# Four matmuls that share one weight load, in a sliding-window matmul on TensorE

## The chip, the cores and the metric

The kernel runs on one core of one Trainium2 chip. The metric is the time of one execution on the device, in microseconds (us); the profile of one execution gives a slightly shorter span, from its first to its last instruction.

## The reference

```python
def reference(x, w, offsets):          # x (4, 4096, 4096) f32, w (4096, 4096) f32
    results = []
    for b in range(4):
        o = int(offsets[b])
        results.append(x[b, o:o+64] @ w)
    return np.stack(results)           # (4, 64, 4096) f32
```

Four windows of 64 rows make 256 rows. They are multiplied by one matrix w of 64 MB. So w is read once, and each part of it is used for only 256 rows.

## The kernel before

The 256 rows are two row halves (g = 0, 1) of 128. They are transposed at the start, so that for each of the 32 k tiles (128 rows of w each) a 128x128 block of xT is the stationary operand ("the weights" in what follows) and w is the moving operand. The output columns are done in two groups (ng) of 2048. Within one group each k tile has 2 row halves times 4 column blocks of 512 columns, that is 8 matmuls into the kernel's 8 PSUM tiles (`bank0` to `bank7` in the program, "banks" below); the four column blocks of a row half use the same weights. Most loads of w (26 of 36) bring two k tiles (1024 KB as f16, from f32) on GpSimd's queue, into 12 rotating buffers.

```python
    def load(ng, ki, n):
        t = wh_pool.tile([P, n * NG], fp16, name="wh", tag="wh")      # 12 buffers
        nc.gpsimd.dma_start(out=..., in_=w[ki * P : (ki + n) * P, ng * NG : (ng + 1) * NG]...)
        for i in range(n):
            wh[(ng, ki + i)] = t[:, i * NG : (i + 1) * NG]
    ...                                       # all loads of w are issued here; x is transposed
    def mm(g, j, ki, rhs, start, stop):
        nc.tensor.matmul(
            out=ps[4 * g + j][:],
            lhsT=xT[g][:, ki * P : (ki + 1) * P],
            rhs=rhs,
            start=start,
            stop=stop,
        )
    ...
    for ng in range(n_ng):
        last = ng == n_ng - 1
        for ki in range(n_k):
            for g in range(G):
                for j in range(n_sub):
                    mm(g, j, ki, wh[(ng, ki)][:, j * NT : (j + 1) * NT], ki == 0, ki == n_k - 1)
        for j in range(n_sub):
            for g in range(G):                # ScalarE evicts half 0, VectorE half 1
                ...
        ...                                   # store both halves
```

## Time and profile before

| | before |
|---|---|
| time | 183.54 us (3 runs, 183.46 to 183.56) |
| span of the profile | 182.0 us |
| TensorE matmuls busy | 122.8 us, 67% |
| weight loads busy (their own track, overlapping the matmuls) | 56.5 us, 31% |
| idle of TensorE ended by a load of w | 32.7 us |

In the profile PE stands for the matmuls of TensorE, PEld for its weight loads, DVE for VectorE, ACT for ScalarE, POOL for GpSimd and SP for SyncE; a q after such a name is that engine's sequencer. "<-" names what ended a wait, and "issue" is time in which an engine waited for nothing that the profile shows. The granted clock, named below, is the share of full speed that TensorE was given.

First the page's two parts on the DMA queues (kind: packets, MB, share of the time of 16 engines) and on the chain of waits that ended last (share of the span, by engine, then by line):

```profile
q0 software_dynamic: 9120, 36.70, 97.0%
...
DMA 88%; issue 3%; POOL 1%; DVE 1%; POOLq 1%; PE 1%; DVEq 0%
DMA wh<-in_w_dram 88%; DVE stage L133 1%; POOL wh L58 1%; PE bank L108 1%; POOLq L72 1%; POOL xrow L79 0%; DVEq L164 0%; POOL identity masks.py:197 0%; POOLq L79 0%; POOLq L58 0%; POOLq masks.py:199 0%; POOLq L153 0%
```

The queue that loads w keeps the DMA engines busy 97% of the time, and the work that ended last is, for 88% of the span, loads of w. Next the groups of instructions of the main loop (busy us, mean ns of one, then the idle time just before them and what ended it):

```profile
L108 PE MATMUL bank<-wh,xT 128*128 128x512 f16 x496 | 112.0, 379 | 32.7 <-DMA wh<-in_w_dram 32.7
L108 PEld LDWEIGHTS <-xT 128*128 128x128 f16 x512 | 49.9, 98 | 98.5 <-issue 42.0
```

There is one weight load (98 ns) for each matmul: 512, of which 496 belong to this matmul group and 16 to the tiles of w that came in another way. The timeline of TensorE shows the rhythm (start, length in us, then the idle time before in brackets):

```profile
41.43 3.61 PE L108 MATMUL bank<-wh,xT 128*128 128x512 f16 x16 [1.28 <-DMA wh<-in_w_dram]
46.40 3.61 PE L108 MATMUL bank<-wh,xT 128*128 128x512 f16 x16 [1.36 <-DMA wh<-in_w_dram]
```

Every 4.9 us two k tiles of w land, TensorE does their sixteen matmuls in 3.61 us, and waits for the next. One matmul is recorded as 0.38 us long, but sixteen take 3.61 us and not 16 x 0.38 = 6.1 us, so their records overlap, and the distance between starts is (3.61 - 0.38) / 15 = 215 ns. Last, the timeline after the last load of w has landed:

```profile
171.26 1.89 PE L108 MATMUL bank<-wh,xT 128*128 128x512 f16 x8 [0.54 <-DMA wh<-in_w_dram]
171.27 1.39 PEld L108 LDWEIGHTS <-xT 128*128 128x128 f16 x7 [0.82 <-issue]
171.68 2.05 ACT L131 COPY stage<-bank 128x512 f32<-128x512 f32 x4 [73.82 <-PE bank L108]
172.54 2.48 DVE L133 COPY stage<-bank 128x512 f32<-128x512 f32 x4 [73.39 <-PE bank L108]
...
175.05 0.38 SPq L135 DMA_DIRECT2D out_dram<-stage  x1
```

Eight matmuls but only seven loads fall in this stretch: the first matmul's weights had been loaded already (a load is recorded at 170.35 us).

### The profile page before, as it was taken

To read this page: it belongs to the slowest core of one execution; us is meant where nothing else is said; L and a number is where in the kernel's file an instruction comes from. 1 tells how busy PE (TensorE), PEld (TensorE's weight loads), DVE (VectorE), ACT (ScalarE), POOL (GpSimd) and SP (SyncE) were. 2 spreads that over 40 slices of the span, in tenths; PEclk is the share of its full clock that TensorE was granted. 3 is DMA by queue.
4 is the path that set the end of the run, shared out by engine and by line. 5 is a ranking of instruction groups with operands and counts; after the bars stand their busy time and mean duration, and the time that the engine had idled before them with its cause. 6 is when DMAs were issued, how large, how long until landed. Compare 5 with 4: busy or idle time off the path is not lost.

```text
span 182.0 us, 1329 instructions
## 1 busy us (share of the span) xinstructions
PE 122.8 (67%) x576; PEld 56.5 (31%) x576; DVE 10.5 (6%) x16; ACT 13.8 (8%) x19; POOL 27.7 (15%) x48
## 2 busy tenths in 40 slices
PE   0004699777777777777988777777777587799700
PEld 0004663333333322333433333333233232343300
DVE  0002540000000000000005000000000000000040
ACT  2081430000000000000004000000000000000210
POOL 4713310111111111110221111111111010100000
PEclk9999999999999999999999999999999999999995
DMA  5999999999999999999999999999999999999995
GB/s 180 348 217 216 206 214 215 216 214 215 212 213 212 216 215 216 214 215 210 212 214 217 215 215 214 212 214 213 215 216 214 215 215 211 214 212 216 367 398 216
DMA packets 9559, 40.97 MB, mean 225 GB/s; under 512 B 722, under 2 KB 722, under 8 KB 8658
## 3 DMA queue, kind: packets, MB, share of 16 engines
q0 software_dynamic: 9120, 36.70, 97.0%
q10 hardware_dynamic: 288, 3.15, 4.6%
q1 hardware_dynamic: 146, 1.05, 1.4%
q8 instruction: 4, 0.07, 0.1%
q14 instruction: 1, 0.01, 0.0%
HBM read 71.30 MB, written 4.19 MB: 415 GB/s over the span
## 4 chain that ended last, share of the span: by engine, by line
DMA 88%; issue 3%; POOL 1%; DVE 1%; POOLq 1%; PE 1%; DVEq 0%
DMA wh<-in_w_dram 88%; DVE stage L133 1%; POOL wh L58 1%; PE bank L108 1%; POOLq L72 1%; POOL xrow L79 0%; DVEq L164 0%; POOL identity masks.py:197 0%; POOLq L79 0%; POOLq L58 0%; POOLq masks.py:199 0%; POOLq L153 0%
## 5 line engine op out<-in xcount | busy, mean ns | idle before, releaser
L108 PE MATMUL bank<-wh,xT 128*128 128x512 f16 x496 | 112.0, 379 | 32.7 <-DMA wh<-in_w_dram 32.7
L108 PEld LDWEIGHTS <-xT 128*128 128x128 f16 x512 | 49.9, 98 | 98.5 <-issue 42.0
L58 POOL DMA_DIRECT2D wh<-in_w_dram x36 | 23.8, 662 | 116.8 <-DMA wh<-in_w_dram 105.8
L94 PE MATMUL bank<-identity,xrow 128*128 128x128 f16 x64 | 7.1, 311 | 17.5 <-DMA xrow<-in_x_dram 17.5
L131 ACT COPY stage<-bank 128x512 f32<-128x512 f32 x8 | 4.1, 599 | 144.4 <-PE bank L108 144.4
L133 DVE COPY stage<-bank 128x512 f32<-128x512 f32 x8 | 5.0, 682 | 145.1 <-PE bank L108 145.1
L94 PEld LDWEIGHTS <-xrow 128*128 128x128 f16 x64 | 6.7, 147 | 17.7 <-issue 17.7
L103 DVE CAST xT<-bank 128x512 f16<-128x512 f32 x8 | 5.5, 691 | 19.4 <-PE bank L94 19.4
L105 ACT CAST xT<-bank 128x512 f16<-128x512 f32 x8 | 4.7, 586 | 7.0 <-PE bank L94 7.0
L108 PE MATMUL bank<-w0half,xT 128*128 128x512 f16 x16 | 4.2, 380 | 0.2 <-DVE stage L133 0.2
L88 ACT CAST w0half<-w0row 128x2048 f16<-128x2048 f32 x1 | 1.9, 1897 | 7.2 <-DMA w0row<-in_w_dram 7.2
L79 POOL DMA_DIRECT2D xrow<-in_x_dram x4 | 2.1, 524 | 2.1 <-issue 2.1
L135 POOL DMA_DIRECT2D out_dram<-stage x2 | 1.1, 536 | 8.2 <-DMA wh<-in_w_dram 8.2
L89 ACT CAST w0half<-w0row 128x2048 f16<-128x2048 f32 x1 | 1.9, 1892 | 0.0
L88 ACT ACT_TABLE_LOAD x1 | 1.3, 1283 | 1.3 <-PEq L153 1.3
masks.py:199 POOL TENSOR_SCALAR_AFFINE_SELECT identity<-identity 128x128 f16<-128x128 f16 x1 | 0.3, 288 | 0.1
masks.py:197 POOL MEMSET identity<- 128x128 f16 x1 | 0.2, 223 | 0.0
L153 POOL MEMSET const-float32-0.0<- 128x1 f32 x1 | 0.1, 99 | 0.4 <-issue 0.4
L153 POOL MEMSET const-uint8-127<- 128x1 uint8 x1 | 0.1, 102 | 0.0
L153 POOL MEMSET const-bfloat16-1.0<- 128x1 bf16 x1 | 0.1, 101 | 0.0
L153 POOL MEMSET const-float32-1.0<- 128x1 f32 x1 | 0.1, 99 | 0.0
## 6 DMA issues: line engine op xcount, KB each, us to landing
wh<-in_w_dram POOLq DMA_DIRECT2D x26, 1024.0 KB, 36.6
wh<-in_w_dram POOLq DMA_DIRECT2D x10, 512.0 KB, 31.3
w0row<-in_w_dram ACTq DMA_DIRECT2D x1, 2048.0 KB, 8.9
xrow<-in_x_dram POOLq DMA_DIRECT2D x4, 512.0 KB, 12.2
out_dram<-stage POOLq DMA_DIRECT2D x2, 1024.0 KB, 22.8
out_dram<-stage ACTq DMA_DIRECT2D x1, 1024.0 KB, 4.9
out_dram<-stage SPq DMA_DIRECT2D x1, 1024.0 KB, 6.0
off_t<-in_offsets_dram SPq DMA_DIRECT2D x1, 0.0 KB
```

What stands on the lines that cost most here:

```text
L58: nc.gpsimd.dma_start(out=t[:].rearrange("p (t n) -> p t n", t=n), in_=w[ki * P : (ki + n) * P, ng * NG : (ng + 1) * NG].rearrange("(t p) ...
L72: o = nc.values_load(off_i32[0:1, 2 * b : 2 * b + 1], engines=[POOL], min_val=0, max_val=S - WIN, skip_runtime_bounds_check_because="offse ...
L79: nc.gpsimd.dma_start(out=x16[g][m * WIN : (m + 1) * WIN, :], in_=x[b][bass.ds(o, WIN), :])
L88: nc.scalar.copy(out=w0_16[:, :NG], in_=w0_32[:, :NG])
L89: nc.scalar.copy(out=w0_16[:, NG:], in_=w0_32[:, NG:])
L94: nc.tensor.matmul(out=ps[t][:, i * P : (i + 1) * P], lhsT=x16[g][:, k * P : (k + 1) * P], rhs=identity[:], start=True, stop=True,)
L103: nc.vector.tensor_copy(out=dst, in_=ps[t][:])
L105: nc.scalar.copy(out=dst, in_=ps[t][:])
L108: nc.tensor.matmul(out=ps[4 * g + j][:], lhsT=xT[g][:, ki * P : (ki + 1) * P], rhs=rhs, start=start, stop=stop,)
L131: nc.scalar.copy(out=dst, in_=ps[4 * g + j][:])
L133: nc.vector.tensor_copy(out=dst, in_=ps[4 * g + j][:])
L135: (q[g] if last else nc.gpsimd).dma_start(out=out[2 * g : 2 * g + 2, :, ng * NG : (ng + 1) * NG], in_=stage[ng][g][:],)
```

## The change

Load each 128x128 block of weights once for the four matmuls that use it. The first matmul of each four is emitted as before; the other three are emitted as instructions that are flagged as not loading weights.

```diff
     def mm(g, j, ki, rhs, start, stop):
-        nc.tensor.matmul(
-            out=ps[4 * g + j][:],
-            lhsT=xT[g][:, ki * P : (ki + 1) * P],
-            rhs=rhs,
-            start=start,
-            stop=stop,
+        out_ap = ps[4 * g + j][:]
+        lhsT = xT[g][:, ki * P : (ki + 1) * P]
+        if j == 0:
+            nc.tensor.matmul(out=out_ap, lhsT=lhsT, rhs=rhs, start=start, stop=stop)
+            return
+        nc.tensor.add_instruction(
+            mybir.InstMatmult(
+                name=nc.get_next_instruction_name(),
+                start_tensor_calc=start,
+                stop_tensor_calc=stop,
+                tile_position=(0, 0),
+                tile_size=(P, P),
+                ldweights=False,
+                ins=[
+                    nc.tensor.lower_ap(rhs, opt=False),
+                    nc.tensor.lower_ap(lhsT, opt=False, for_matmul_weights=True),
+                ],
+                outs=[nc.tensor.lower_ap(out_ap)],
+            )
         )
```

## The prediction

> **What bounds the kernel now.** Loading w does. The chain of waits that ended last (182.0 us span) is 88% loads of w; TensorE matmuls of the main loop are about 1% of it. The queue table gives the software queue 97% of the DMA engines' time, and the stages between 26 and 171 us move a flat 214 to 226 GB/s (destination bytes) at a DMA share above 1. TensorE is the follower: in the timeline each 1 MB load (two k tiles) lands every 4.9 us, TensorE runs its sixteen matmuls in 3.61 us and then idles 1.23 to 1.36 us, ended each time by the next load. In all it idles 32.7 us in 30 waits for loads.
>
> **What the change removes.** 384 of 512 weight loads in the main loop, 98 ns each in the line table: about 37.5 of 49.9 us of busy time on the weight-load track. It adds nothing: same matmuls, order, banks, buffers and DMAs.
>
> **What that is worth.** Nothing on TensorE, because the loads are already hidden. Sixteen matmuls in 3.61 us, with 0.38 us for one, is (3.61-0.38)/15 = 215 ns from start to start, although every one has its own load; the last group of eight gives (1.89-0.38)/7 = 216 ns. In that last group the first matmul starts at 171.26 us with its weights already loaded; the load recorded at 171.27 us belongs to the second. [...]a full-array load fits under each matmul.
>
> **How much is on the critical path.** After the last load lands (171.22 us): five matmuls (1.25 us), four VectorE evictions (about 2.5 us) and the last store (6.0 us to landing). Only the five matmuls could shrink, at a 215 ns pitch set by 512 columns; I expect under 0.05 us. Even if TensorE gained, it would wait longer for w. If instead the fifth matmul's load were exposed (four shared matmuls not letting the next load go ahead), a group would lose about 0.1 us, 0.2 us per k tile, 0.4 us per pair against 1.23 us of idle: still hidden, and about 0.1 us at the tail.
>
> **Prediction.** 183.5 us, 8 in 10 between 182.9 and 184.2. Faster by over 2%: 0.01; within 2%: 0.97; slower by over 2%: 0.02.
>
> **What would show the steps.** Right: weight loads of the main loop x128, busy near 12.5 us; matmul mean still about 379 ns; sixteen matmuls still 3.6 us; idle before matmuls still about 32 us, ended by loads of w; last load lands near 171.2 us; chain still 88% loads. Wrong: groups of sixteen at 3.2 us or less (loads did cost something), or above 3.8 us (sharing exposes loads), or a changed DMA rate.
>
> **What would make it wrong.** A lower granted clock[...]: it is 1.00 in every stage from 26 to 171 us, and at half of it sixteen matmuls would take an estimated 15x0.43+0.6 = 7 us (twice the measured pitch), more than the 4.9 us between loads; TensorE would then bind and the kernel be some 40% slower. [...] Or matmuls without a load waiting for the whole preceding matmul, which would need over 80 ns extra per matmul (1.3 us of idle over sixteen) before the time moved.

The forecast's sum was the time of the kernel before, 183.5 us, less nothing on TensorE and less under 0.05 us in the tail (estimate). The half clock in its last paragraph is one that the profile before shows: 0.50 from 180 to 182 us, with no matmul after 173.2 us. That the distance between starts goes with the columns was measured later: 215 ns for 512, 55.7 for 128 and 29.1 for 64 (experiments 7 to 10).

## The result, and the profile after

The changed kernel takes 183.52 us (median of 6 runs, 183.44 to 183.64), the kernel before 183.55 us beside it (6 runs). The ratio is 1.000, with a 95% interval of 0.9987 to 1.0012. Here and below a ratio is the mean time of one kernel's runs over that of the other's in the same rounds, so it is not quite the ratio of the medians quoted. Executions over 1.5% slower than the fastest of the same kernel are left out of the means.

The page after, the chain of waits that ended last:

```profile
DMA 88%; issue 3%; POOL 1%; DVE 1%; POOLq 1%; PE 1%; DVEq 0%
```

The time is as predicted, and so is the chain. But the groups of the main loop are not (line 111 is the first matmul of each four, line 113 the other three):

```profile
L113 PE MATMUL bank<-wh,xT 128*128 128x512 f16 x372 | 100.4, 379 | 0.0
L111 PE MATMUL bank<-wh,xT 128*128 128x512 f16 x124 | 46.9, 378 | 32.4 <-DMA wh<-in_w_dram 32.4
L113 PEld LDWEIGHTS <-xT 128*128 128x128 f16 x384 | 37.5, 98 | 82.8 <-issue 41.3
L111 PEld LDWEIGHTS <-xT 128*128 128x128 f16 x128 | 12.5, 98 | 15.6 <-issue 0.8
```

Line 113 has 384 weight loads: the very loads that the change was to remove. 384 + 128 = 512, as before. The timeline shows them between the matmuls:

```profile
41.41 0.38 PE L111 MATMUL bank<-wh,xT 128*128 128x512 f16 x1 [1.28 <-DMA wh<-in_w_dram]
41.41 0.53 PEld L113 LDWEIGHTS <-xT 128*128 128x128 f16 x3 [1.56 <-issue]
41.62 0.81 PE L113 MATMUL bank<-wh,xT 128*128 128x512 f16 x3
...
42.05 0.10 PEld L111 LDWEIGHTS <-xT 128*128 128x128 f16 x1
```

So the change removed nothing. The listings of the two built programs say why. While the kernel is being written down there is no separate load instruction in the program at all; when the tile context closes, a pass splits each of the 576 matmuls (64 for the transposes, 512 in the main loop) into a load and a matmul that doesn't load, and it does so for the 384 that carry the flag already. Both built programs then hold 576 loads and 576 matmuls. With source line numbers left out, the two listings (all five engines, operands and waits included) are the same line for line:

```
before                                    after
L108 Matmult bank_78<-wh,xT_76 128x512    L111 Matmult bank_78<-wh,xT_76 128x512
L108 Ldweights xT_76                      L113 Ldweights xT_76
L108 Matmult bank_79<-wh,xT_76 128x512    L113 Matmult bank_79<-wh,xT_76 128x512
L108 Ldweights xT_76                      L113 Ldweights xT_76
L108 Matmult bank_80<-wh,xT_76 128x512    L113 Matmult bank_80<-wh,xT_76 128x512
```

The measured "same" is therefore a comparison of a program with itself. It says nothing yet about what sharing a load is worth. The experiments make the change for real.

### The profile page after: what moved, and what is told of

It is laid out like the page before. It is cut to its first block, busy times and chain, and to the rows that moved or that the text cites. A ratio compares the mean times of both kernels' runs of the same rounds, so it can differ in the third digit from the quotient of the medians.

```text
span 182.0 us, 1329 instructions
## 1 busy us (share of the span) xinstructions
PE 123.0 (68%) x576; PEld 56.6 (31%) x576; DVE 10.5 (6%) x16; ACT 13.8 (8%) x19; POOL 27.6 (15%) x48
## 3 DMA queue, kind: packets, MB, share of 16 engines
HBM read 71.30 MB, written 4.19 MB: 415 GB/s over the span
## 4 chain that ended last, share of the span: by engine, by line
DMA 88%; issue 3%; POOL 1%; DVE 1%; POOLq 1%; PE 1%; DVEq 0%
DMA wh<-in_w_dram 88%; DVE stage L146 1%; POOL wh L58 1%; POOLq L72 1%; POOL xrow L79 0%; PE bank L113 0%; PE bank L111 0%; DVEq L177 0%; POOL identity masks.py:197 0%; POOLq L79 0%; POOLq L58 0%; POOLq masks.py:199 0%; POOLq L166 0%
## 5 line engine op out<-in xcount | busy, mean ns | idle before, releaser
L113 PE MATMUL bank<-wh,xT 128*128 128x512 f16 x372 | 100.4, 379 | 0.0
L111 PE MATMUL bank<-wh,xT 128*128 128x512 f16 x124 | 46.9, 378 | 32.4 <-DMA wh<-in_w_dram 32.4
L111 PEld LDWEIGHTS <-xT 128*128 128x128 f16 x128 | 12.5, 98 | 15.6 <-issue 0.8
L113 PE MATMUL bank<-w0half,xT 128*128 128x512 f16 x12 | 3.7, 385 | 0.2 <-DVE stage L146 0.2
L111 PE MATMUL bank<-w0half,xT 128*128 128x512 f16 x4 | 1.8, 442 | 0.0
```

The source lines that it names most:

```text
L111: nc.tensor.matmul(out=out_ap, lhsT=lhsT, rhs=rhs, start=start, stop=stop)
L113: nc.tensor.add_instruction(mybir.InstMatmult(name=nc.get_next_instruction_name(), start_tensor_calc=start, stop_tensor_calc=stop, tile_po ...
```

## The experiments

### 1. The loads really taken out

After the tile context has closed, the loads of weights that are held already are removed from the program's list; the kernel itself is the one before. None of those removed carried a wait or a signal, which the edit asserts.

```diff
     with _tile.TileContext(nc) as tc:
         tile_sliding_window_matmul_kernel(tc, *args)
+    n_cut = 0
+    for blk in nc.main_func.blocks:
+        keep, held = [], None
+        for i in blk.instructions:
+            if type(i).__name__ == "InstLdweights":
+                key = str(i.ins[0].memref) + str(i.ins[0].offset)
+                if key == held and "xT" in key:
+                    assert not (i.sync_info and (i.sync_info.on_wait or i.sync_info.on_update))
+                    n_cut += 1
+                    continue
+                held = key
+            keep.append(i)
+        blk.instructions = keep
+    assert n_cut == 384, n_cut
```

> The kernel before, with 384 of the 512 main-loop weight loads really taken out of the finished program (the changed kernel still ran all 512). Theory A (loads are hidden under the matmuls and TensorE waits for w anyway): 128 main-loop loads in the trace, about 12.5 us busy; sixteen matmuls still 3.61 us, matmul mean 379 ns; idle before matmuls about 32 us; time 183.5 us, within 0.3 us of before. Rival B (a load delays its matmul): sixteen matmuls below 3.5 us, idle time grows by the same amount, time still about 183.5 because the last load of w lands at the same time, at most 0.1 us less at the tail. Rival C (four matmuls on shared weights keep the next load from going ahead): sixteen matmuls about 3.9 us. Rival D (weight loads help to hold the clock): granted clock below 1.00 between 26 and 171 us, matmuls start 0.43 us apart, time over 250 us. Rival E: the back end puts the loads back, 512 in the trace.

Measured: correct, 183.44 us (5 runs, 183.29 to 183.58) against 183.50 us; ratio 0.9997 (0.9983 to 1.0010). The groups, and the timeline of one pair of k tiles:

```profile
L108 PE MATMUL bank<-wh,xT 128*128 128x512 f16 x496 | 111.9, 379 | 32.3 <-DMA wh<-in_w_dram 32.3
...
L108 PEld LDWEIGHTS <-xT 128*128 128x128 f16 x128 | 12.5, 98 | 135.1 <-issue 135.1
```

```profile
41.32 3.61 PE L108 MATMUL bank<-wh,xT 128*128 128x512 f16 x16 [1.15 <-DMA wh<-in_w_dram]
41.97 0.10 PEld L108 LDWEIGHTS <-xT 128*128 128x128 f16 x1 [2.08 <-issue]
42.83 0.10 PEld L108 LDWEIGHTS <-xT 128*128 128x128 f16 x1 [0.77 <-issue]
43.69 0.10 PEld L108 LDWEIGHTS <-xT 128*128 128x128 f16 x1 [0.77 <-issue]
44.56 0.10 PEld L108 LDWEIGHTS <-xT 128*128 128x128 f16 x1 [0.77 <-issue]
```

Now there are 128 loads, one for four matmuls, 0.86 us apart. The sixteen matmuls still take 3.61 us, TensorE still waits 32.3 us for w, and the granted clock is 1.00 from 26 to 171 us as before. Theory A holds and rivals B, C, D and E fall: no cost of a load shows (3.61 us with 16 loads and with 4), the next load still starts while the matmuls before it run (at 41.97 us, with the sixteen running from 41.32 to 44.93 us), and the granted clock was 1.00 with 128 loads as with 512. The weight loads' busy share of the span went from 31% to 11% (56.5 us of 182.0 us, and 19.2 of 181.9) with no change in time.

### 2 and 3. TensorE made the bottleneck, with and without the loads

In the kernel before, a small cost of a load could hide in TensorE's idle time. So each group of four matmuls is done twice, and the eviction halves the result; now TensorE has more to do than the loads of w leave time for. Experiment 3 is the same with the redundant loads cut as in experiment 1.

```diff
-            for g in range(G):
+            for g in [0, 1, 0, 1]:            # start on the first visit of a bank, stop on the second
...
-                    nc.scalar.copy(out=dst, in_=ps[4 * g + j][:])
+                    nc.scalar.mul(out=dst, in_=ps[4 * g + j][:], mul=0.5)      # likewise on VectorE
```

> Every group of four matmuls is done twice (result halved at the eviction, so still right), all 1024 matmuls with a load of their own: TensorE needs about 7.1 us per pair of k tiles against 4.9 us between loads of w, so TensorE binds. Start of the main loop 24.3 us, 1024 matmuls at 216 ns = 221 us, about 10 us of eviction and last store: 255 us (250 to 262). If the load costs its own time (98 ns) on TensorE, the matmuls would start 314 ns apart and the time be about 355 us; the trace of before says not.

> As the doubled kernel, with 768 of its 1024 loads taken out, one load for four matmuls. TensorE binds here, so what a load costs shows at once, 768 times. Theory A (hidden): same time as the doubled kernel within 0.5%, matmuls 215 to 216 ns apart. Rival B (each load costs some ns): faster by 768 times the cost; [...]20 ns each 15 us. Rival C (sharing exposes the next load): slower by 256 times up to 98 ns, up to 25 us.

Measured: 256.03 us with all loads (4 runs, 254.00 to 256.17), 254.39 us with the loads cut (4 runs, 254.06 to 255.42), both correct; ratios to the kernel before 1.3917 and 1.3859. Timeline of TensorE and group of its loads, first with all loads, then with 768 cut:

```profile
24.31 4.19 PE L108 MATMUL bank<-w0half,xT 128*128 128x512 f16 x16
28.33 107.22 PE L108 MATMUL bank<-wh,xT 128*128 128x512 f16 x496
...
L108 PEld LDWEIGHTS <-xT 128*128 128x128 f16 x1024 | 100.4, 98 | 121.6 <-issue 1.7
```

```profile
24.12 3.62 PE L108 MATMUL bank<-w0half,xT 128*128 128x512 f16 x16
27.57 107.22 PE L108 MATMUL bank<-wh,xT 128*128 128x512 f16 x496
...
L108 PEld LDWEIGHTS <-xT 128*128 128x128 f16 x256 | 25.0, 98 | 195.6 <-issue 195.6
```

496 matmuls in a row, without a gap, take 107.22 us in both. That run of matmuls has 496 loads in the one and 124 in the other. A difference as small as 0.01 us over the 372 missing loads would show, so a load costs less than 0.03 ns (0.01 / 372) in these two profiles. The 0.8 us by which the two profiled spans differ arose before this point: the first sixteen matmuls took 4.19 us in one and 3.62 us in the other, and the run of 496 starts at 28.33 and 27.57 us. The loads are not needed for such a slow start: the sixteen matmuls on w0half, whose first eight start the main loop there, have a mean of 416 ns in experiment 1, with the loads cut, and of 380 ns in the kernel before, with all of them. The executions of one kernel differ by as much (254.00 and 256.17 us with all loads), so that is not put down to the loads.

### 4. More loads than before

This is the changed kernel with an explicit load ahead of each four and the flag on all four matmuls. It is what one would write to say "one load, four matmuls" outright, but the pass adds its own load to each matmul all the same.

```diff
         if j == 0:
-            nc.tensor.matmul(out=out_ap, lhsT=lhsT, rhs=rhs, start=start, stop=stop)
-            return
+            nc.tensor.ldweights(lhsT)
```

> The changed kernel with one explicit load ahead of each group of four and the flag on all four matmuls: the program then has 640 main-loop loads, 128 more than before. Theory A: hidden where two loads fit under one matmul (2 x 98 = 196 ns below 215 ns), at most a few ns more per group; sixteen matmuls below 3.7 us, time 183.5 us. Rival B: each extra load costs about 0.1 us, sixteen matmuls 4.0 us, still hidden behind the loads of w, time 183.5 to 183.7 us.

Measured: correct, 183.44 us (4 runs) against 183.50 us, ratio 0.9997 (0.9981 to 1.0012); 640 loads in the main loop, sixteen matmuls still 3.61 us. The timeline of the weight-load track:

```profile
41.62 0.10 PEld L111 LDWEIGHTS <-xT 128*128 128x128 f16 x1
41.66 0.70 PEld L112 LDWEIGHTS <-xT 128*128 128x128 f16 x4
```

The explicit load starts at 41.62 us and the next one 40 ns later, though each is recorded as 0.10 us long. The 98 ns are thus the length of a load's record, not how long it keeps the next one away.

### 5 and 6. Is loading w really what binds?

Experiment 5 does column block 0 of each row half twice, twenty matmuls where there were sixteen. Experiment 6 leaves out every second k tile of w and uses the tile before it in its place; its result is wrong.

```diff
 # experiment 5
-                for j in range(n_sub):
+                for j in [0, 0, 1, 2, 3]:     # bank of block 0 halved at the eviction
 # experiment 6
...                                            # tile 31 uses tile 0, which is loaded in any case
             if (ng, ki) not in wh:
-                load(ng, ki, 2 if ki < n_k - 4 - (ki % 2) else 1)
+                load(ng, ki, 1)
+                wh[(ng, ki + 1)] = wh[(ng, ki)]
```

> The kernel before with column block 0 of each row half done twice (its bank halved at the eviction, still right): twenty matmuls per pair of k tiles instead of sixteen, each with a load. Theory A (TensorE has 1.2 to 1.36 us to spare in each 4.9 us): twenty matmuls take 19 x 0.216 + 0.38 = 4.5 us, idle before matmuls falls from 32 to about 6 to 10 us, time 183.5 to 184.0 us (the tail has at most two matmuls more ahead of its last eviction, 0.4 us). Rival: if TensorE were on the critical path, 126 more matmuls at 216 ns would add up to 27 us.

> Wrong on purpose: every second k tile of w is not loaded, its matmuls use the tile before it; all 512 matmuls with their loads stay. If loading w binds, the time falls until TensorE binds: 24.3 us to the main loop, 512 matmuls at 216 ns = 111 us, 10 us of tail: 146 us (140 to 155). If TensorE or anything else but the loads of w bound the kernel, it stays near 183.5 us.

Measured: 183.59 us for experiment 5 (4 runs), correct, ratio 1.0006 (0.9990 to 1.0023); 143.5 us for experiment 6 (one run, state unknown, wrong as meant). The group of matmuls in experiment 5:

```profile
L108 PE MATMUL bank<-wh,xT 128*128 128x512 f16 x620 | 137.1, 379 | 8.1 <-DMA wh<-in_w_dram 8.1
```

A quarter more work on TensorE costs no time: it went into the idle time, which fell from 32.7 to 8.1 us. Little of that time is left: the chain that ended last is now 67% DMA and 24% TensorE. And with half the loads of w the chain that ended last turns to TensorE (in experiment 6 its lines have moved by one):

```profile
PE 77%; DMA 10%; DVE 3%; issue 3%; POOLq 1%; DVEq 0%; POOL 0%
```

So loading w bounds the kernel before, and TensorE comes next.

### 7 and 8. Matmuls of 128 columns

Does a load show when its matmul is short? Each matmul of 512 columns is cut into four of 128, each with a load of its own; experiment 8 cuts the 1920 redundant ones. Theory A2 was that load and matmul partly add up. The 54 ns in A1 are a quarter of the 215 ns.

```diff
+        for c in range(0, NT, NARROW):                          # NARROW = 128
             nc.tensor.matmul(
-                out=ps[4 * g + j][:],
+                out=ps[4 * g + j][:, c : c + NARROW],
                 lhsT=xT[g][:, ki * P : (ki + 1) * P],
-                rhs=rhs,
-                start=start,
-                stop=stop,
+                rhs=rhs[:, c : c + NARROW],
+                start=start and c == 0,
+                stop=stop and c == NT - NARROW,
```

> Each 512-column matmul of the main loop cut into four of 128 columns, each with its own load of the same weights: 2048 loads and 2048 matmuls, same arithmetic. Loads no longer fit easily: a load's record is 98 ns, though two loads of the run with more loads began only about 42 ns apart. Theory A1 (a load is hidden whenever it is shorter than the matmul, 128 columns = 54 to 56 ns against about 42): sixteen old matmuls still about 3.6 us, time 183.5 us. [...]Theory A3 (they add up, 42 + 56 = 98 ns): 2048 x 98 = 201 us + 34 us = about 235 us.

> The narrow kernel with 1920 of its 2048 loads taken out, one for sixteen matmuls of 128 columns. Under A2 and A3 TensorE is freed: 64 x 56 ns = 3.6 us per pair below 4.9 us, time back at 183.5 us, and the gain over the narrow kernel is what sharing is worth where loads show. Under A1 no difference from the narrow kernel.

Measured: 184.76 us with all loads (4 runs, ratio 1.0067) and 184.66 us with the loads cut (4 runs, ratio 1.0055), both correct. One pair of k tiles in the timeline, with the loads and without:

```profile
41.42 3.73 PE L110 MATMUL bank<-wh,xT 128*128 128x128 f16 x64 [1.23 <-DMA wh<-in_w_dram]
41.43 3.61 PEld L110 LDWEIGHTS <-xT 128*128 128x128 f16 x64 [1.35 <-issue]
```

```profile
41.45 3.73 PE L110 MATMUL bank<-wh,xT 128*128 128x128 f16 x64 [1.16 <-DMA wh<-in_w_dram]
```

64 matmuls take 3.73 us in both, which with 0.22 us for one is (3.73 - 0.22) / 63 = 55.7 ns from start to start. A1 holds: even at 128 columns, with starts 55.7 ns apart, a load recorded as 98 ns costs nothing (3.73 us with 64 loads and with 4). Both narrow kernels are about 1.2 us slower than the kernel before, and in both the last load of w lands later (172.37 against 171.22 us). In each trace it is one load of w that comes about 1 us late, before 106.14 us in experiment 7 and as the last one in experiment 8. Why was not tested; the loads of weights are not the cause, since it is there without them.

### 9 and 10. Matmuls of 64 columns

The same with NARROW = 64: 4096 matmuls, with 4096 loads or with 128.

> Each 512-column matmul of the main loop cut into eight of 64 columns, each with its own load: 4096 loads and 4096 matmuls. At 128 columns a load was still free (64 matmuls in 3.73 us with and without, 55.7 ns apart). A matmul of 64 columns takes an estimated 55.7/2 = 28 ns; two loads of the run with more loads began 42 ns apart, so the load should now set the pitch: 128 x 42 = 5.4 us per pair of k tiles against 4.9 us between loads of w, TensorE binds, 4096 x 42 = 172 us + 34 us = about 206 us (195 to 225), and idle before matmuls nearly gone. If the load were hidden even here, the pair would take about 3.6 to 3.8 us and the time be 184 to 187 us[...].

> The 64-column kernel with 3968 of its 4096 loads taken out, one for 32 matmuls. If the load set the pitch, TensorE is freed: 128 x 28 = 3.6 us per pair, idle before matmuls back near 30 us, time 184 to 187 us, some 10% below the 64-column kernel with loads: the case in which the change pays. If the matmuls of 64 columns are limited by their own issue (above 38 ns each), TensorE still binds and the gain is smaller or none.

Measured: 211.49 us with all loads (4 runs, ratio 1.1537, 1.1517 to 1.1557), 185.85 us with the loads cut (4 runs, ratio 1.0120, 1.0100 to 1.0139), both correct. Here cutting the loads is worth 12%. The sizes are near what was expected, but the reason expected is wrong, so the near hit is luck. The timeline of TensorE with all loads, with the line of its weight-load track for the same stretch:

```profile
42.77 3.89 PE L110 MATMUL bank<-wh,xT 128*128 128x64 f16 x128 [2.58 <-issue]
42.77 3.80 PEld L110 LDWEIGHTS <-xT 128*128 128x128 f16 x128 [2.67 <-issue]
...
117.50 1.04 PE L110 MATMUL bank<-w0half,xT 128*128 128x64 f16 x30
120.57 1.15 PE L110 MATMUL bank<-w0half,xT 128*128 128x64 f16 x34 [2.03 <-issue]
...
180.06 21.68 PE L110 MATMUL bank<-wh,xT 128*128 128x64 f16 x738 [0.93 <-issue]
```

and with the loads cut:

```profile
41.45 3.89 PE L110 MATMUL bank<-wh,xT 128*128 128x64 f16 x128 [1.00 <-DMA wh<-in_w_dram]
```

128 matmuls take 3.89 us in both, with 0.19 us for one (3.89 - 0.19) / 127 = 29.1 ns from start to start. Loads that start (3.80 - 0.10) / 127 = 29.1 ns apart still do not slow the matmuls. What costs the time is that TensorE stands still, mostly for 2.0 to 2.6 us, after every 128 matmuls up to 180 us, for nothing that the profile shows ("issue"): 26 waits, 46.0 us in all. It is not a wait for w: one of the gaps falls between the 30th and the 34 other matmuls of a tile that had been in the buffer since the start. And the gaps end at 180 us, after which 738 matmuls run without one. 128 matmuls with 128 loads are 256 instructions, and the queue table of this run has 32 instruction packets with 0.52 MB, that is 16 KB each; the kernel before has 4 packets and 7168 instructions fewer (1024 matmuls and loads in the main loop against 8192), which is 256 instructions for each of the 28 more packets. With the loads cut there are 17. The queue lines of experiments 9 and 10:

```profile
q8 instruction: 32, 0.52, 0.9%
q8 instruction: 17, 0.28, 0.5%
```

### 11. What the gaps of the 64-column kernel are

In experiment 9 there is a 16 KB instruction packet for every 256 instructions, and a gap after every 128 matmuls with their 128 loads. The author's estimate from these counts was that the gaps are waits for the packets, which come late while the loads of w fill the DMA engines (DMA share 1.06 from 26 to 171 us). If so, the gaps should go when the loads of w go. Experiment 11 is the 64-column kernel with all its weight loads, with half the loads of w as in experiment 6 (wrong).

> The 64-column kernel with all its loads, but every second k tile of w not loaded (wrong on purpose, as in the half-bytes run), to tell what its gaps are. In its trace 128 matmuls took 3.89 us with loads as without (29 ns apart), yet TensorE then stood idle 2.0 to 2.6 us for nothing the profile shows, once per 128 loads and 128 matmuls; the queue table has 32 instruction packets of 16 KB[...]; and the gaps were gone for the last 738 matmuls, when the loads of w had ended. Theory F (the gaps are instruction fetch queued behind the loads of w): here the loads of w end near 95 us; gaps before that, none after; from then on about 29 ns per matmul, so 24.3 + 68 us with gaps (some 1470 matmuls at 5.92 us per 128) + 2600 x 0.0294 = 77 us + 10 us: about 180 us. Rival G (TensorE cannot issue more than 256 instructions in 5.92 us): gaps all the way, 211 us. Rival H (the gaps are waits for w that the profile does not show): with half the loads none anywhere, about 155 us.

Measured: 179.03 us (one run, state unknown, wrong as meant); expected about 180. The timeline of TensorE:

```profile
49.45 5.39 PE L111 MATMUL bank<-wh,xT 128*128 128x64 f16 x128 [2.03 <-issue]
55.37 3.89 PE L111 MATMUL bank<-wh,xT 128*128 128x64 f16 x128 [0.53 <-issue]
...
81.97 21.68 PE L111 MATMUL bank<-wh,xT 128*128 128x64 f16 x738 [2.58 <-issue]
...
127.64 40.03 PE L111 MATMUL bank<-wh,xT 128*128 128x64 f16 x1314 [2.85 <-issue]
```

and busy times by stretch (PE, PEld, DVE, ACT, POOL with counts, then granted clock, DMA share, GB/s):

```profile
49.50:51.50 2.00, 2.00 (x39) 2.00 (x39) 0.00 (x0) 0.00 (x0) 0.00 (x0) 0.50 1.09 219
...
124.00:128.00 4.00, 1.15 (x39) 1.05 (x35) 0.00 (x0) 0.00 (x0) 0.00 (x0) 0.98 1.02 423
...
132.00:165.00 33.00, 33.00 (x1138) 33.00 (x1134) 0.00 (x0) 0.00 (x0) 0.00 (x0) 1.00 0.02 4
```

While the DMA engines are full (DMA share 1.06, 212 GB/s from 26 to 60 us) there is a gap after every 128 matmuls; from there to 124 us, with a thinner stream of w (0.68, 109 GB/s from 60 to 92 us), some boundaries have a gap and most have none (738 matmuls run through from 81.97 us); at 124 to 128 us, with 423 GB/s, there is one of 2.85 us; and where the DMA engines are idle (4 GB/s) TensorE runs 33 us without one, with the same mix of loads and matmuls. Rival G, a limit of issue, would have kept the gaps to the end, and rival H would have had none. One part of the expectation failed: the loads of w did not end near 95 us, but ran on to about 128 us in a thinner stream, since they waited for buffers (17 waits of GpSimd for TensorE, 74.6 us).

After some gaps the clock was lower: the 128 matmuls at 49.45 us took 5.39 us and not 3.89, and by stretch the granted clock was 0.50 from 49.5 to 51.5 us. In experiment 9 five groups of 128 took 5.37 to 5.44 us, after gaps of 2.03 to 2.30 us, though others after the same gaps took 3.89; in the kernel before, with its regular gaps of 1.23 to 1.36 us, the clock was 1.00 from 26 to 171 us. At 49.45 us the lower clock cost no time: the gap after these 128 was 0.53 us instead of 2.03, and the next group started 5.92 us after theirs. Experiment 9 has the same distance with the lower clock (groups at 54.88 and 60.80 us) and at full clock (60.80 and 66.72 us). At 127.64 us, where the last loads of w were ending (granted clock 0.59 from 128 to 132 us), the lower clock did cost an estimated 1.6 us: 1314 matmuls took 40.03 us and not 1313 x 29.1 ns + 0.19 us = 38.4 us.

The views do not print when an instruction packet arrives, but the trace files hold it. All 26 gaps of experiment 9 and all 11 of this run that the profile puts down to "issue" end 1.2 to 1.6 us after a 16 KB instruction packet has landed. In experiment 9 these packets start 5.7 to 6.4 us apart up to 173 us and 3.3 to 3.7 us apart from 178 us on, when the DMA engines are nearly idle (DMA share 0.02, 5 GB/s from 180 to 201 us); a group of 128 needs 3.73 us without a gap (128 x 29.1 ns). In experiments 7 and 10, with about half the instructions, the packets start 7.5 to 10.8 us apart, and the profile puts no wait of a matmul down to "issue". So the author takes the gaps for waits for instructions. That the packets come late because they queue behind the loads of w fits all of this, but what a packet waits for is not in the trace.

## Why the prediction was right or wrong

- **The time and its range were right** (183.5 predicted, 183.52 measured), and so was the forecast of no change. As a test of the argument this agreement was luck: the measurement could not have been anything else, because the built program was the same. It was earned only by experiment 1, which made the change and measured 183.44 us.
- **"What the change removes: 384 of 512 weight loads" was wrong, and is the step that failed.** It removed none. The step was read off the diff and taken for granted; the profile shows 384 loads at line 113. The prediction's own sign for it, "weight loads of the main loop x128, busy near 12.5 us", is met by line 111 alone, and the sum over both lines, 512, refutes it.
- **"Nothing on TensorE, because the loads are already hidden" was right**, and was shown by the experiments and not by the result: sixteen matmuls take 3.61 us with 16 loads, with 4 and with 20 (experiments 1 and 4), and where TensorE binds 496 matmuls take 107.22 us with 496 loads or 124 (experiments 2 and 3).
- **"TensorE is the follower" was right**: 25% more matmuls cost nothing, and half the bytes of w brought 143.5 us (experiments 5 and 6).
- **The tail: "under 0.05 us"**: with the loads really cut, the median is 0.06 us below that of the kernel before (183.44 against 183.50 us), inside the spread of either. It can't be told from zero.
- **The feared case, a lower clock without the loads, did not occur**: it is 1.00 from 26 to 171 us in experiment 1 as well. The feared exposed fifth load did not occur either.

## What to carry to other kernels

After a change that should remove instructions, count them in the profile or in the built program before any time is compared, adding up all the source lines that can make them; a pass may have put them back. In these runs a weight load under a running matmul took no time of TensorE, down to 64 columns (29.1 ns from start to start with the loads and without), so look at the start-to-start distance of the matmuls and not at the busy time of the loads. But a load is also an instruction: with 64 columns and full DMA engines, cutting the loads took the instruction packets from 32 to 17, TensorE's "issue" gaps from 26 to none, and the time from 211.49 to 185.85 us (experiments 9 and 10). And a faster TensorE does not pay while it waits for a 4.9 us load with 3.61 us of work.
